# Opening the second feed-forward of a two-layer prefix-DiT: row sums on VectorE, weight remainders on GpSimd, a written-out order, and the two scale folds at set places

## The chip, the cores and the metric

One core of a Trainium2 chip runs the whole program, one launch per execution. The metric is the device time of one execution in microseconds (us). TensorE (PE in the profile) multiplies, VectorE (DVE), ScalarE (ACT) and GpSimd (POOL) do the elementwise work, SyncE (SP) issues the loads.

## What is computed

The model has two layers on 512 latent tokens (and 256 context tokens in the first layer), width 1024. Layer 0 mixes by attention, layer 1 by a gated recurrence (HGRN2); each mixer is followed by a SwiGLU feed-forward. Cut to what the change touches, which is the step from layer 1's mixer to its feed-forward:

```python
def rms_norm(x, w):
    y = x * lax.rsqrt(jnp.mean(x * x, axis=-1, keepdims=True) + NORM_EPS)
    return y * w
def modulate(h, shift, scale):
    return h * (1.0 + scale) + shift
def swiglu(h, w_in, w_out):              # w_in: 1024 x 5632, w_out: 2816 x 1024
    a, u = jnp.split(h @ w_in, 2, axis=-1)
    return (jax.nn.silu(a) * u) @ w_out
...
        h = h + gt1_l * y_l              # y_l ends with the product o @ w_o of the mixer
        h = h + gt2_l * swiglu(modulate(rms_norm(h, norm_ffn_w[i]), sh2_l, sc2_l),
                               ffn_w_in[i], ffn_w_out[i])
```

All inputs are float32.

## The kernel before, in words

**Layout.** Activations lie transposed: `hT[o]` is block o of eight, 128 channels on the partitions by tokens along the free axis. The 512 latent tokens of layer 1 are worked in two halves of H = 256 tokens, called half 0 and half 1.

**Products in three parts.** A float32 product is made of three products of a narrower type. `split` (L88) cuts an operand into a high part (a cast on ACT, L90) and a remainder, the low part (a subtraction on DVE or POOL, L95). `mm3` (L116) then issues high by high (L118), high by low of the moving operand (L119; the profile shows it as weight high with x low) and weight low by x high (L120).

**What stands at the change.** `hgrn_wo_last` (L1821) makes the last two of eight parts of the mixer's output product. For each half of the tokens it makes eight output rows, one per block o; in half 0 six of the rows have 3 matmuls left and two have 6, in half 1 each of the eight has 6, every matmul 256 tokens wide. Each row ends in `residual` (L760), one DVE instruction that reads the row from PSUM, scales it and adds it to `hT[o]`. It is a generator: each `next(pre)` emits one row.

`start_recurrence` (L1393), called once for layer 1, draws these rows and opens the feed-forward between them. For each half:

- **squares**: for each row, ACT squares the new `hT[o]` half (L274 for the first row, L278 for the others) and POOL adds the square to the running sum `acc_n` (L279), through two buffers, `sw`;
- **first fold** `rstd_cols` (L281): PE sums `acc_n` over its partitions (L285, tile `ssq`, two 128-token columns), DVE scales (L292), POOL raises to the power -1/2 (L294, tile `rc`);
- **second fold** `rstd_psum` (L297): DVE puts the 256 factors on diagonals (L300), PE multiplies them with ones (L304, tile `rstd`), so that each factor stands on all partitions in PSUM;
- **x** by `xhalf` (L1028): per block k, DVE multiplies `hT[k]` with the norm's weight and `rstd` (L1033), ACT adds the shift (L1035), ACT casts the high part and DVE (odd k) or POOL (even k) subtracts the low part; tiles `xw` for half 0, `xb12` and `xb22` for half 1;
- **products**: `plain(ps, j, i, k, h, ...)` (L1039) adds block k of hidden block j, i = 0 for the part under silu and 1 for the factor, to the PSUM tile `ffi`; three matmuls of 256 tokens each;
- **hidden** `plain_hidden` (L1055): silu on ACT, multiplication on DVE, and a split.

The weights of hidden blocks 0 and 1 come as four raw tiles (j, i) of 128 x 1024, loaded by SP into four ring buffers; `plain_split` (L1016) splits each. The low part of (0,0) is on POOL, those of (0,1), (1,0) and (1,1) on DVE. The order of the products in the program is: (0,0) and (0,1) of half 0 block by block, then (1,0) and (1,1) of half 0, then half 1.

**What sets the order.** A scheduler orders each engine's instructions when the kernel is built: by their place in the program, but an instruction whose inputs are ready earlier by the scheduler's own timing may go ahead. `pin(ins)` (L122) holds one instruction behind the one that was written before it on the same engine. Each engine then works its own list strictly in order and waits at the head of it. In the kernel before, the low parts of three weights are pinned here, and almost nothing else; the rows, the squares, the sums, the folds and x are placed by the scheduler.

## Time and profile before

| | |
|---|---|
| median of 3 runs | 1802.78 us (1802.26 to 1803.30) |
| the profiled execution's own time | 1803.39 us |
| its span in the profile | 1801.6 us |
| PE busy, of the span | 1747.4 us (97%) |
| DVE, ACT, POOL busy | 1306.6, 870.9, 641.0 us |
| mean granted PE clock | 0.993 |
| last row's product before the first fold, to the first product of x | 1424.57 to 1433.84 us |
| first product of half 1 | 1449.90 us |

Times inside the profile are counted from the start of the span. The profiled execution took 1803.39 us, 1.8 us more than its span and 0.6 us more than the median; a change in the span is taken as the same change in the time. In a row of the timeline stand: start, duration, engine, line, operation, output and inputs, shape, count, and in brackets the idle time before it with what ended it. A start is when the instruction began by the record; where an instruction then had to wait for a resource inside the chip, the wait lies within its duration. Rows with a count above 1 are merged neighbours. In a table of windows stand: the stretch, its length, the busy time of PE, PEld, DVE, ACT and POOL with the number of instructions, the granted PE clock (1.00 is full), and the DMA's share and rate.

### The profile page before, as it was taken

What the parts mean: (1) busy time and instruction counts of PE and PEld (TensorE: products, weight loads), DVE (VectorE), ACT (ScalarE), POOL (GpSimd) and SP (SyncE); (2) the same over time, 40 slices, a digit from 0 to 9 for tenths busy, and PEclk for the clock granted to TensorE, in tenths of its full rate; (3) what the DMA queues carried; (4) which work ended last, traced back from release to release, by engine and by line L of the source; (5) the groups of instructions that cost most, each with busy time, mean ns of one, the idle gap of its engine ahead of it and who ended that gap; (6) DMA issues with size and microseconds to landing.
All of it is one profiled execution on the core that took longest, in us unless ns stands there. A gap on an engine that the chain in (4) does not pass through costs nothing.

```text
span 1801.6 us, 30622 instructions
## 1 busy us (share of the span) xinstructions
PE 1747.4 (97%) x11717; PEld 1603.7 (89%) x11717; DVE 1306.6 (73%) x2269; ACT 870.9 (48%) x1777; POOL 641.0 (36%) x582
## 2 busy tenths in 40 slices
PE   9989999999999999999999999999999899999998
PEld 6788788998899989999998999898898899999996
DVE  4876688888988788888766555655747658786764
ACT  3544777767433514243446433334334545554544
POOL 1453445434513314132303243224425454333420
PEclk9999999999999999999999999999999899999999
DMA  9534400002134242545331212123211123333322
GB/s 339 177 114 139 142 25 24 25 1 77 36 111 118 65 135 83 164 132 161 94 106 46 70 61 77 54 71 94 71 48 47 56 59 115 100 115 100 100 61 83
DMA packets 213458, 166.43 MB, mean 92 GB/s; under 512 B 7952, under 2 KB 190400, under 8 KB 213312
## 3 DMA queue, kind: packets, MB, share of 16 engines
q1 hardware_dynamic: 213024, 163.43, 29.6%
q8 instruction: 92, 1.51, 0.3%
q10 hardware_dynamic: 288, 1.05, 0.1%
q14 instruction: 54, 0.44, 0.1%
HBM read 162.36 MB, written 2.10 MB: 91 GB/s over the span
## 4 chain that ended last, share of the span: by engine, by line
PE 77%; DVE 9%; ACT 4%; POOL 4%; issue 3%; DMA 2%; SPq 0%; POOLq 0%; DVEq 0%; ACTq 0%
PE ffo L120 5%; PE ffo L118 5%; PE ffo L119 5%; PE x L118 3%; PE x L120 3%; PE x L119 3%; PE pt L787 3%; PE lv L1716 3%; PE y L120 2%; PE y L118 2%; PE y L119 2%; PE hz L118 2%; PE hz L119 2%; PE hz L120 2%; PE sc L729 1%
## 5 line engine op out<-in xcount | busy, mean ns | idle before, releaser
L1723 POOL TENSOR_TENSOR KD<-KD,tot 128x384 f32<-128x384 f32 x96 | 102.3, 1088 | 81.7 <-ACT kc L1706 78.0
L777 POOL TENSOR_SCALAR pf<-pf,st 128x768 f32<-128x768 f32 (+1 forms) x96 | 73.3, 766 | 126.0 <-DVE st L776 89.5
L760 DVE SCALAR_TENSOR_TENSOR hT<-ffo,modc,hT 128x512 f32<-128x512 f32 (+1 forms) x122 | 78.6, 649 | 45.1 <-PE ffo L120 45.1
L120 PE MATMUL ffo<-gh,wlo_w 128*128 128x512 f32 (+1 forms) x304 | 102.7, 338 | 0.0
L119 PE MATMUL ffo<-gl,whi_w 128*128 128x512 f32 (+1 forms) x304 | 102.3, 336 | 0.0
L118 PE MATMUL ffo<-gh,whi_w 128*128 128x512 f32 (+1 forms) x304 | 101.8, 338 | 0.0
L242 DVE SCALAR_TENSOR_TENSOR adacc<-adw,csil,adacc 128x512 f32<-128x512 f32 x98 | 83.4, 861 | 8.9 <-DMA adw<-in_ada_w_dram 8.8
L95 DVE TENSOR_TENSOR ptl<-pt,pth 128x384 fp32r<-128x384 f32 (+1 forms) x160 | 79.9, 524 | 12.8 <-ACT pth L90 11.6
L90 ACT CAST pth<-pt 128x384 fp32r<-128x384 f32 (+1 forms) x160 | 69.7, 460 | 34.2 <-PE pt L787 22.4
L775 ACT ACTIVATE pf<-sc,st 128x768 f32<-128x768 f32 (+1 forms) x96 | 73.3, 764 | 18.9 <-DVE st L773 18.0
L1723 DVE TENSOR_TENSOR QD<-QD,tot 128x256 f32<-128x256 f32 x96 | 52.5, 587 | 41.4 <-PE lv L1716 41.2
L773 DVE TENSOR_REDUCE st<-sc 128x1 f32<-128x768 f32 (+1 forms) x96 | 74.1, 773 | 10.1 <-PE sc L730 8.7
L1706 ACT COPY kc<-KD 128x256 f32<-128x256 f32 x112 | 43.4, 414 | 75.6 <-PE lv L1716 46.2
L787 PE MATMUL pt<-ident,pf 128*128 128x128 f32 x448 | 72.1, 275 | 5.2 <-DVE ptl L95 3.8
L118 PE MATMUL ffo<-gh,foh 128*128 128x512 f32 (+1 forms) x186 | 71.5, 384 | 0.0
L120 PE MATMUL ffo<-gh,fol 128*128 128x512 f32 (+1 forms) x186 | 70.9, 381 | 0.2 <-DVE fol L95 0.2
L119 PE MATMUL ffo<-gl,foh 128*128 128x512 f32 (+1 forms) x186 | 70.9, 381 | 0.0
L1782 POOL TENSOR_SCALAR oss<-oss 128x4 f32<-128x4 f32 (+1 forms) x9 | 4.7, 523 | 182.8 <-DVE oss L1781 182.7
L1716 PE MATMUL lv<-QD,kc 128*128 128x128 f32 x448 | 64.1, 288 | 4.5 <-DVE QD L1723 2.4
L1716 PEld LDWEIGHTS lv<-QD,kc 128*128 128x128 f32 x448 | 59.5, 194 | 8.5 <-issue 4.3
L787 PEld LDWEIGHTS pt<-ident,pf 128*128 128x128 f32 x448 | 51.3, 140 | 13.8 <-issue 6.4
L119 PEld LDWEIGHTS ffo<-gl,whi_w 128*128 128x128 f32 x304 | 57.3, 188 | 6.8
(1114 smaller groups left out, 6801.7 us busy)
## 6 DMA issues: line engine op xcount, KB each, us to landing
adw<-in_ada_w_dram SPq DMA_DIRECT2D x40, 512.0 KB, 4.6
adw<-in_ada_w_dram SPq DMA_DIRECT2D x80, 256.0 KB, 3.0
raw_hz<-in_hgrn_w_in_dram SPq DMA_DIRECT2D x14, 512.0 KB, 3.7
adr<-in_ada_w_dram SPq DMA_DIRECT2D x16, 256.0 KB, 5.1
adr<-in_ada_w_dram SPq DMA_DIRECT2D x8, 512.0 KB, 8.5
raw_wq<-in_attn_w_qkv_dram SPq DMA_DIRECT2D x8, 512.0 KB, 4.9
raw_wo<-in_attn_w_o_dram SPq DMA_DIRECT2D x8, 512.0 KB, 3.4
raw_hv<-in_hgrn_w_in_dram SPq DMA_DIRECT2D x8, 512.0 KB, 4.6
```

What stands on the lines that cost most here:

```text
L95: m = (eng or DVE).tensor_tensor(lo, src, hi.bitcast(F32), op=ALU.subtract)
L118: PE.matmul(ps, ahi, bhi, start=first, stop=False, **kw)
L119: PE.matmul(ps, ahi, blo, start=False, stop=False, **kw)
L120: PE.matmul(ps, alo, bhi, start=False, stop=last, **kw)
L242: pin(DVE.scalar_tensor_tensor(a, raw, cc, a, op0=ALU.mult, op1=ALU.add))
L760: DVE.scalar_tensor_tensor(hT[o][:, a:e], ps, mcol(layer, ch, o, v), hT[o][:, a:e], op0=ALU.mult, op1=ALU.add)
L773: DVE.tensor_reduce(st3[:, 0:1], ps[:, :nk], op=ALU.max, axis=AX.X, negate=True)
L775: ACT.activation(pf, ps[:, :nk], AF.Exp, bias=st3[:, 0:1], accum_out=st3[:, 1:2])
L777: POOL.tensor_scalar(pf, pf, st3[:, 2:3], 1.0, op0=ALU.mult, op1=ALU.mult)
L787: PE.transpose(pt[:, i * P : (i + 1) * P], pf[:, (i0 + i) * P : (i0 + i + 1) * P], ident)
L1716: PE.matmul(ps[:, cs], kc[:, cs], mv, start=True, stop=True)
L1723: eng.tensor_tensor(view, view, f, op=ALU.mult)
```

## The change

- The squares of rows 1 to 7 of each half go to a new tile with three buffers, and the adding moves from POOL to DVE. It is written one or more rows behind: an add stands behind a later `residual` on DVE. Squares, adds, residuals are all pinned.
- The low parts of (0,1), (1,0) and (1,1) move from DVE to POOL, each cut into two instructions of 512 columns, and pinned.
- The first fold of half 0 is written after row 3 of half 1, the second after row 5; both are pinned on all their engines. Row starts of half 1 are pinned on PE.
- x of half 0 is written with its parts apart: the multiplication, the shift and the cast (`xfirst`), and one block later the low part (`xlow`), which is always on DVE, all pinned. Blocks 0 to 2 stand among rows 5 to 7, blocks 3 to 7 and the last two squares and five adds of half 1 stand among the products.
- The first fold of half 1 is written after the products (1,0) of half 0, the second after five of the eight blocks of (1,1).
- The second `plain_hidden` and the splits of weight block 2 are pinned.

```diff
@@ -113,9 +113,11 @@
-    def mm3(ps, ahi, alo, bhi, blo, first, last, onto=False):
+    def mm3(ps, ahi, alo, bhi, blo, first, last, onto=False, late=False):
         kw = dict(skip_group_check=True) if onto else {}
-        PE.matmul(ps, ahi, bhi, start=first, stop=False, **kw)
+        m = PE.matmul(ps, ahi, bhi, start=first, stop=False, **kw)
+        if late:
+            pin(m)
...
@@ -1013,36 +1021,60 @@
...
-        def plain_split(j, i, late=""):
+        def plain_split(j, i, late="", eng=None):
...
             pool_ = (j, i) == (0, 0) or j > 1 and i if layer else j == 0
-            split(t[0], t[1], raws.pop(("w", j, i)), POOL if pool_ else DVE, late=late)
+            raw = raws.pop(("w", j, i))
+            if eng is None:
+                split(t[0], t[1], raw, POOL if pool_ else DVE, late=late)
+            else:
+                ACT.copy(t[0], raw)
+                for c in (slice(0, 512), slice(512, 1024)):
+                    pin(eng.tensor_tensor(t[1][:, c], raw[:, c], t[0][:, c].bitcast(F32), op=ALU.subtract))
...
+        def xfirst(k, h, late=False):
             if k not in x:
                 x[k] = gslot((10 if layer else 2) + k, F32, f"x{k}")
             a0, e0 = halves[h][0][1], halves[h][-1][2]
             for v, a, e in halves[h]:
-                DVE.scalar_tensor_tensor(x[k][:, a:e], hT[k][:, a:e], a_c[:, k, v : v + 1], rst[h][:, a - a0 : e - a0],
-                                         op0=ALU.mult, op1=ALU.mult)
-                ACT.activation(x[k][:, a:e], x[k][:, a:e], AF.Identity, bias=mcol(layer, 3, k, v))
+                m = DVE.scalar_tensor_tensor(x[k][:, a:e], hT[k][:, a:e], a_c[:, k, v : v + 1], rst[h][:, a - a0 : e - a0],
+                                             op0=ALU.mult, op1=ALU.mult)
+                if late:
+                    pin(m)
+                m = ACT.activation(x[k][:, a:e], x[k][:, a:e], AF.Identity, bias=mcol(layer, 3, k, v))
+                if late:
+                    pin(m)
+            if late:
+                pin(ACT.copy(xops[("b1" if k < 4 else "b2") + "12"[h]][0][:, k % 4], x[k][:, a0:e0]))
+
+        def xlow(k, h):
+            a0, e0 = halves[h][0][1], halves[h][-1][2]
             xh, xl = xops[("b1" if k < 4 else "b2") + "12"[h]]
-            split(xh[:, k % 4], xl[:, k % 4], x[k][:, a0:e0], DVE if k % 2 else POOL)
-
-        def plain(ps, j, i, k, h, first, last):
+            pin(DVE.tensor_tensor(xl[:, k % 4], x[k][:, a0:e0], xh[:, k % 4].bitcast(F32), op=ALU.subtract))
+
+        def xsecond(k, h, eng):
+            a0, e0 = halves[h][0][1], halves[h][-1][2]
+            xh, xl = xops[("b1" if k < 4 else "b2") + "12"[h]]
+            split(xh[:, k % 4], xl[:, k % 4], x[k][:, a0:e0], eng)
...
@@ -1396,52 +1432,82 @@
             order = [0, 4, 1, 5, 2, 6, 3, 7]
             ps = [[{}, {}] for _ in range(nplain)]
 
-            def products(j, h, i, ks):
+            def products(j, h, i, ks, late=False):
                 for k in ks:
-                    plain(ps[j][i], j, i, k, h, k == 0, k == KT - 1)
-
-            for h in range(2):
+                    plain(ps[j][i], j, i, k, h, k == 0, k == KT - 1, late and k == ks[0])
+
+            sums = []
+
+            def square(h, o):
                 hs = slice(h * H, (h + 1) * H)
-                for i in range(KT):
-                    o = next(pre)
-                    sumsq_add(acc_n[:, hs], fp, hT[o][:, hs], o, i == 0, POOL, tag="sw", bufs=2, width=512)
-                    if h == 0 and i == 0:
-                        plain_split(0, 0, "l")
-                    if h == 0 and i == KT - 1:
-                        plain_split(0, 1, "l")
-                    if h == 1 and i == 1:
-                        plain_split(1, 0, "l")
-                    if h == 1 and i == 2:
-                        rst[0] = rstd_psum(ctile("c22", 2), rc[0], H)
-                    if h == 1 and i >= 4:
-                        xhalf(i - 4, 0)
-                rc[h] = rstd_cols(fp, acc_n[:, hs], H, f"rc{h}")
+                if o == 0:
+                    pin(ACT.activation(acc_n[:, hs], hT[o][:, hs], AF.Square))
+                    return
+                sq = fp.tile([P, H], F32, tag="sqo", bufs=3, name="sqo")
+                pin(ACT.activation(sq, hT[o][:, hs], AF.Square))
+                sums.append((acc_n[:, hs], sq))
+
+            def add():
+                acc, sq = sums.pop(0)
+                pin(DVE.tensor_tensor(acc, acc, sq, op=ALU.add))
+
+            plain_split(0, 0, "l")
+            for i in range(KT):
+                square(0, next(pre))
+                if len(sums) > 1:
+                    add()
+                if i in (1, 4):
+                    plain_split(*((0, 1) if i == 1 else (1, 0)), "l", POOL)
+            for i in range(KT):
+                o = next(pre)
+                if i == 0:
+                    add()
+                if i < 6:
+                    square(1, o)
+                if i == 3:
+                    rc[0] = rstd_cols(fp, acc_n[:, 0:H], H, "rc0", late=True)
+                    plain_split(1, 1, "l", POOL)
+                if i in (3, 4):
+                    add()
+                if i == 5:
+                    rst[0] = rstd_psum(ctile("c22", 2), rc[0], H, late=True)
+                if i >= 5:
+                    xfirst(i - 5, 0, True)
+                if i == KT - 1:
+                    xlow(0, 0)
             for _ in pre:
                 pass
             for _ in range(2):
                 load_next()
             for k in range(KT):
-                if k >= 4:
-                    xhalf(k, 0)
+                if 0 < k < 6:
+                    xfirst(k + 2, 0, True)
+                if k < KT - 1:
+                    xlow(k + 1, 0)
+                if k in (1, 3):
+                    square(1, 6 if k == 1 else 7)
+                if 0 < k < 6:
+                    add()
                 for i in range(2):
                     products(0, 0, i, [k])
-            plain_split(1, 1, "l")
-            rst[1] = rstd_psum(ctile("c22", 2), rc[1], H)
+            hidden_tiles(0)
+            hidden_tiles(1)
+            products(1, 0, 0, range(KT))
+            rc[1] = rstd_cols(fp, acc_n[:, H:n], H, "rc1", late=True)
+            products(1, 0, 1, range(5), True)
+            rst[1] = rstd_psum(ctile("c22", 2), rc[1], H, late=True)
+            products(1, 0, 1, range(5, KT), True)
             for k in order[:2]:
                 xhalf(k, 1)
-            hidden_tiles(0)
-            hidden_tiles(1)
-            for i in range(2):
-                products(1, 0, i, range(KT))
             plain_hidden(0, 0, *ps[0])
             for k in order[2:]:
                 xhalf(k, 1)
-            plain_hidden(1, 0, *ps[1])
+            plain_hidden(1, 0, *ps[1], late=True)
             for i_, k in enumerate(order):
                 for i in range(2):
                     plain(ps[0][i], 0, i, k, 1, i_ == 0, i_ == KT - 1)
-            plain_split(2, 0)
-            plain_split(2, 1, "l")
+            plain_split(2, 0, "hl")
+            plain_split(2, 1, "hl")
...
@@ -1850,8 +1916,8 @@
                     ps, todo = both[:, (o - 6) * 256 : (o - 6) * 256 + 256], (0, 1)
                 for i in todo:
                     mm3(ps, wo[i][0][:, osl], wo[i][1][:, osl], os_[i][0][:, a:e], os_[i][1][:, a:e],
-                        i == 0, i == 1, True)
-                residual(o, ps, 1, 2, 0, a, e)
+                        i == 0, i == 1, True, h == 1 and i == 0)
+                pin(residual(o, ps, 1, 2, 0, a, e))
                 yield o
 
     NSTEP = 14
```

What is cut from the diff passes `late` on to the folds and to `plain_hidden`, so that their instructions are pinned, and returns the instruction of `residual`.

More of the change, by code (lines that the diff above doesn't have):

```diff
@@ L287, in rstd_cols, with rstd_of @@
                 pin(m)
-        return rstd_of(pl, pc, nt, tag)
-    def rstd_of(pl, pc, nt, tag="rc"):
+        return rstd_of(pl, pc, nt, tag, late)
+    def rstd_of(pl, pc, nt, tag="rc", late=False):
         rc = pl.tile([P, NT], F32, tag=tag, name="rc")[:, :nt]
-        DVE.tensor_scalar(rc, pc[:, 0 : 2 * nt].rearrange("p (t v) -> p t v", v=2)[:, :, 0], 1.0 / D, EPS,
+        m = DVE.tensor_scalar(rc, pc[:, 0 : 2 * nt].rearrange("p (t v) -> p t v", v=2)[:, :, 0], 1.0 / D, EPS,
                           op0=ALU.mult, op1=ALU.add)
-        POOL.tensor_tensor(rc, rc, mhalf.to_broadcast([P, nt]), op=ALU.pow)
+        if late:
+            pin(m)
+        m = POOL.tensor_tensor(rc, rc, mhalf.to_broadcast([P, nt]), op=ALU.pow)
+        if late:
+            pin(m)
         return rc
@@ L299, in rstd_psum @@
         dg = dg[:, 0:n].rearrange("p (t q) -> p t q", q=P)
-        DVE.tensor_tensor(dg, ident.unsqueeze(1).to_broadcast([P, nt, P]), rc.unsqueeze(2).to_broadcast([P, nt, P]),
+        m = DVE.tensor_tensor(dg, ident.unsqueeze(1).to_broadcast([P, nt, P]), rc.unsqueeze(2).to_broadcast([P, nt, P]),
                           op=ALU.mult)
+        if late:
+            pin(m)
         ps = bank("rstd")[:, 0:n]
@@ L759, in residual @@
     def residual(o, ps, layer, ch, v, a, e):
-        DVE.scalar_tensor_tensor(hT[o][:, a:e], ps, mcol(layer, ch, o, v), hT[o][:, a:e], op0=ALU.mult, op1=ALU.add)
+        return DVE.scalar_tensor_tensor(hT[o][:, a:e], ps, mcol(layer, ch, o, v), hT[o][:, a:e], op0=ALU.mult, op1=ALU.add)
     ap_ = pool("att", att)
@@ L1028, in xhalf @@
         def xhalf(k, h):
+            xfirst(k, h)
+            xsecond(k, h, DVE if k % 2 else POOL)
+        def xfirst(k, h, late=False):
             if k not in x:
@@ L1044, in plain @@
                 ps[h] = xbank("ffi")[:, 0:H]
-            mm3(ps[h], hi[:, c], lo[:, c], xh[:, k % 4], xl[:, k % 4], first, last)
+            mm3(ps[h], hi[:, c], lo[:, c], xh[:, k % 4], xl[:, k % 4], first, last, late=late)
         gh, gl = {}, {}
@@ L1053, in hidden_tiles, with plain_hidden @@
             gl[j] = gslot(at + 1, F32R, f"gl{jj}")
-        def plain_hidden(j, h, psa, psu):
+        def plain_hidden(j, h, psa, psu, late=False):
             c = ctile("c22", 2)
-            ACT.activation(c, psa[h], AF.Silu)
-            DVE.tensor_tensor(c, psu[h], c, op=ALU.mult)
-            split(gh[j][:, h * H : h * H + H], gl[j][:, h * H : h * H + H], c)
+            m = ACT.activation(c, psa[h], AF.Silu)
+            if late:
+                pin(m)
+            m = DVE.tensor_tensor(c, psu[h], c, op=ALU.mult)
+            if late:
+                pin(m)
+            split(gh[j][:, h * H : h * H + H], gl[j][:, h * H : h * H + H], c, late="hl" if late else "")
         def xsplit(m, i, src, eng=DVE, late=""):
```

6 lines of the change are left out of this document (added).

## The prediction

> **What bounds the kernel now.** I read the page first, then who PE waited for from 1390 to 1520 us, then a table of windows, then the timeline there.
>
> ```profile
> PE 1747.4 (97%) x11717; PEld 1603.7 (89%) x11717; DVE 1306.6 (73%) x2269; ACT 870.9 (48%) x1777; POOL 641.0 (36%) x582
> ```
>
> PE carries the kernel, so a change pays only where PE is idle or slowed. In the opening it waits four times, and the windows show that the first wait costs more than its length:
>
> ```profile
> PE ssq L285 <- POOL acc_n L279: 3.2, 1, 3.2
> PE ffi L118 <- ACT xw L90: 1.8, 1, 1.8
> PE ffi L119 <- POOL xw L95: 0.6, 1, 0.6
> PE ffi L119 <- DVE xw L95: 0.3, 1, 0.3
> ```
>
> ```profile
> 474.78:478.19 3.41, 2.65 (x8) 2.42 (x9) 3.19 (x6) 2.27 (x5) 0.00 (x0) 0.50 0.00 0
> 478.19:481.61 3.42, 3.38 (x11) 2.57 (x10) 2.61 (x6) 3.09 (x8) 0.00 (x0) 0.50 0.52 153
> 1382.73:1386.14 3.41, 1.82 (x8) 0.95 (x7) 3.41 (x4) 1.02 (x3) 2.88 (x3) 1.00 0.24 70
> 1386.14:1389.55 3.41, 3.41 (x17) 3.41 (x17) 3.41 (x9) 0.59 (x1) 0.18 (x1) 0.50 0.30 89
> 1423.69:1427.10 3.41, 1.15 (x10) 0.95 (x8) 1.30 (x2) 1.92 (x5) 3.17 (x4) 1.00 0.59 172
> 1427.10:1430.51 3.41, 2.44 (x11) 2.44 (x12) 0.96 (x4) 0.89 (x3) 2.36 (x5) 0.50 0.47 135
> 1430.51:1433.93 3.42, 1.65 (x9) 1.35 (x7) 2.63 (x8) 2.12 (x6) 2.35 (x4) 0.50 0.01 2
> 1433.93:1437.34 3.41, 3.41 (x16) 3.41 (x17) 2.79 (x8) 3.10 (x10) 2.98 (x5) 0.50 0.00 0
> 1437.34:1440.75 3.41, 2.93 (x25) 2.72 (x23) 1.41 (x4) 2.46 (x9) 1.87 (x4) 1.00 0.00 0
> ```
>
> The granted clock holds one value per slice of 3.41 us. A slice in which PE was busy 1.82 us or less is followed by one at 0.50; one at 0.50 with 2.65 us busy (474.78) is followed by another at 0.50, one with 3.41 us (1433.93) is not. Here three slices run at half speed. PE is busy 2.44 + 1.65 + 3.41 = 7.5 us in them, and half of that, 3.75 us, is lost. With the waits, 5.9 us, the opening holds 9.7 us (0.5%) to be won at most. What can be told from no change by a measurement of this kernel is about 0.2%, 3.6 us.
>
> Where the first wait comes from:
>
> ```profile
> 1417.81 1.04 ACT L90 CAST w01h<-raw_('w', 0, 1)_14886 128x1024 fp32r<-128x1024 f32 x1
> 1418.74 1.05 ACT L90 CAST w11h<-raw_('w', 1, 0)_14888 128x1024 fp32r<-128x1024 f32 x1
> 1418.34 3.83 DVE L760 SCALAR_TENSOR_TENSOR hT<-hwo,modc,hT 128x256 f32<-128x256 f32 x9
> 1419.69 0.42 ACT L274 ACTIVATE acc_n<-hT 128x256 f32<-128x256 f32 x1
> 1420.01 0.71 ACT L278 ACTIVATE sq<-hT 128x256 f32<-128x256 f32 x2
> 1420.49 8.21 POOL L279 TENSOR_TENSOR acc_n<-acc_n,sq 128x256 f32<-128x256 f32 x8 [2.23 <-ACT sq L278]
> 1428.07 1.01 PE L285 MATMUL ssq<-ones,acc_n 128*128 128x2 f32 x4 [3.23 <-POOL acc_n L279]
> ```
>
> Residuals follow each other at 3.83 / 9, about 0.4 us; POOL's adds take 8.21 / 8 = 1.03 us, and PE stands before the fold for 3.23 us, from 1424.84 to 1428.07. Its idle time ends when the sum does.
>
> **The change, part by part.** *The sums.* On DVE an add of two SBUF tiles has the form of a low part: 0.41 us, the next 0.33 us later. But that is its price alone:
>
> ```profile
> 1448.64 0.41 DVE L95 TENSOR_TENSOR xb12l<-x,xb12h 128x256 fp32r<-128x256 f32 x1
> 1448.97 0.42 DVE L95 TENSOR_TENSOR xb22l<-x,xb22h 128x256 fp32r<-128x256 f32 x1
> 1451.13 2.65 POOL L95 TENSOR_TENSOR wlo_w<-raw_('w', 2, 1)_15083,whi_w 128x1024 fp32r<-128x1024 f32 x1
> 1451.44 2.62 DVE L95 TENSOR_TENSOR xb22l<-x,xb22h 128x256 fp32r<-128x256 f32 x1
> 1415.87 2.39 POOL L95 TENSOR_TENSOR wlo_w<-raw_('w', 0, 0)_14884,whi_w 128x1024 fp32r<-128x1024 f32 x1
> ```
>
> The same low part that took 0.42 us took 2.62 us when POOL's weight remainder had begun 0.3 us before it, and ended 0.28 us after that one ended. So the two exclude each other for a whole instruction. Residuals do not: nine ran at 0.4 us each while POOL was adding. The change puts just this beside the adds: four POOL halves of 2.39 / 2 = 1.2 us for (0,1) and (1,0), free to start when their casts end, at 1418.85 and 1419.79.
>
> The Trainium skill (SBUF — State Buffer, Who interferes with whom) has it as a rule: a DVE instruction with two SBUF inputs and a GpSimd one that reads SBUF hold the shared port one at a time, and the second blocks until the first ends; it speaks against this change, and the 2.62 us agree.
>
> DVE's list is now residual 0, 1, 2, add 1, residual 3, add 2 and so on. Square 1 ends at 1420.43 and add 1 is next, but POOL is in its second half (1420.1 to 1421.3): add 1 at 1421.3. Behind a waiting add stand the next residual and ACT's next square; PE's rows wait for neither. POOL's third half then takes 1421.6 to 1422.85, add 2 follows; the fourth ends at 1424.4, add 3 follows, at 1424.7. Then four more residual-and-add pairs of 0.4 + 0.335, 2.9 us: the sum stands at **1427.7**, 0.3 us before now. Without exclusion it would stand at 1425.4. I take 1427.7, because the exclusion is in the rows; both ends stay.
>
> PE meets this earlier than before. The fold stands after row 3 of half 1: 30 + 24 row matmuls from 1417.15 (the first after the last head's product) at 0.1175 us end at 1423.5. The wait is 4.2 us for 3.2, and the slice 1423.69 to 1427.10 is empty, so the clock falls again.
>
> *From the first fold to x.* Prices, at half speed where it is PE:
>
> ```profile
> 1417.15 0.71 PE L118 MATMUL hwo<-oth,whi_hwo 128*128 128x256 f32 x4
> 1449.78 0.28 PE L120 MATMUL ffi<-xw,w11l 128*128 128x256 f32 x1
> 1449.90 0.28 PE L118 MATMUL ffi<-xb12h,whi_w 128*128 128x256 f32 x1
> 1430.16 0.41 PE L120 MATMUL hwo<-oth,wlo_hwo 128*128 128x256 f32 x1
> 1430.37 0.41 PE L118 MATMUL hwo<-oth,whi_hwo 128*128 128x256 f32 x1
> 1429.36 0.71 POOL L294 TENSOR_TENSOR rc<-rc,mhalf 128x2 f32<-128x2 f32 x1 [0.66 <-DVE rc L292]
> 1430.10 0.43 DVE L300 TENSOR_TENSOR c<-ident,rc 128x256 f32<-128x256 f32 x1 [0.43 <-POOL rc L294]
> 1431.01 1.06 PE L304 MATMUL rstd<-c,ones 128*128 128x128 f32 x4
> 1432.11 0.48 DVE L1033 SCALAR_TENSOR_TENSOR x<-hT,a_ffn,rstd 128x256 f32<-128x256 f32 x1 [0.79 <-PE rstd L304]
> 1433.84 0.58 PE L118 MATMUL ffi<-xw,whi_w 128*128 128x256 f32 x1 [1.77 <-ACT xw L90]
> ```
>
> Now 4.0 us lie between fold and x (1428.07 to 1432.11). After: the first fold 0.8, rows 4 and 5, twelve matmuls at 0.213 = 2.6, so row 5 ends at about 1431.5; its residual, pinned ahead of the diagonals, 0.5; the diagonals 0.43 with up to 0.6 of waiting for a POOL half of (1,1), which starts right after the power: 1432.9; the second fold 1.06: **x at 1433.9**. The pinned residual hides the power's 0.71, but itself costs the path. Rows 6 and 7, twelve more at 0.213, stand behind the second fold and hold PE until 1436.4; products of x begin there, where they began at 1433.84.
>
> *Products of half 0.* DVE now does per block x 0.4, low part 0.335 and add 0.335 = 1.07 us; the low part of block 7 ends at 1444.5. On ACT the two late squares lie between casts; a block costs ACT 0.40 + 0.30 and has 1.07, so they are hidden, at 0.3 us each if it had not. PE has 72 matmuls, 8.5 us, in the same 8 us when (1,0) is drawn forward, so DVE's price is hidden, and PE's own work decides: from 1437.9 (x 1 and 2 wait on DVE behind the residuals of rows 6 and 7, then comes the first low part) 94 matmuls, 11.0, and two folds, 0.9, make 1449.8 at full clock. The clock recovers at 1437.34, at 1440.75 or at 1444.2, by whether the 2.8 us or so of busy time in a slice are enough (the rows leave that open between 2.65 and 3.41); half of the time from 1437.9 is lost. So (1,1) ends at 1449.8, 1451.2 or 1452.9; now it ends at 1449.90, where half 1 begins. Taken: the middle one, **+1.3 us**, since 2.8 is nearer to 2.65 in the first slice and the next is full.
>
> *Second fold of half 1.*
>
> ```profile
> 1444.14 0.61 PE L304 MATMUL rstd<-c,ones 128*128 128x128 f32 x4
> 1447.03 0.91 ACT L1035 ACTIVATE x<-x,modc 128x256 f32<-128x256 f32 x2
> 1447.84 0.39 ACT L90 CAST xb12h<-x 128x256 fp32r<-128x256 f32 x1
> 1446.59 0.75 POOL L95 TENSOR_TENSOR xb12l<-x,xb12h 128x256 fp32r<-128x256 f32 x1 [4.92 <-ACT xb12h L90]
> ```
>
> Now this fold is 5.8 us ahead of half 1's first product (1449.90), and x of half 1 is made under (1,0) and (1,1). After, nine matmuls, 1.06 us, are left behind it. From its start to the first low part: 0.61 + 0.48 + 0.51 + 0.39 + 0.75 and four hand-overs of about 0.05 = 2.9 us, against 1.5 of PE work, the fold's own and the nine. PE then takes a block in 0.7 us, ACT makes one in 0.40 + 0.30, so it doesn't catch up: **+1.4 us**. Zero would need x earlier than its fold; the upper end is 4 us, if DVE takes x and low parts in the written order, where four blocks' low parts wait 1.0 us each (0.51 + 0.39 and hand-overs) for their cast, with the next x behind them.
>
> *The rest.* The 512-column cut, the third buffer and the pins add no work. Casts of (2,0) and (2,1) move behind the second hidden block, but their product begins about 11 us later than half 1's, against a cast of 1.05 and a remainder of 2.65: nothing. If that cover were gone they would cost 3.7. The loads of (2,0) to (3,1) follow the freed raw tiles: (2,1) now follows POOL's (0,1), 3 us earlier; nobody waits. Removed from DVE are three remainders of 1.2 us, which now hide no more than the waits of the adds.
>
> Sum: 1.3 + 1.4 = +2.7 us on 1803.39 is 1806.1; the profiled execution lies 0.6 above the median, so **1805.5**.
>
> **Rivals.** *A: POOL is not in the way* (its halves run earlier, or yield). The sum stands at 1425.4. For: POOL is idle from 1418.26 (1415.87 + 2.39) to 1420.49. Against: the casts end at 1418.85 and 1419.79. PE then waits 1.9 us, the slice to 1427.10 is busy 1.5 us, less than 1.82, and the clock falls at 1427.10, when most of rows 4 and 5 is done: x at 1429.7, rows 6 and 7 to 1432.1, the first low part at 1433.6, then 11.9 of work and 1.9 for half speed until 1437.34: 1447.4, -2.5 + 1.4 = -1.1, **1801.7**. *B: A, and the clock stays.* The sum comes half a microsecond sooner, or the slices lie otherwise; rows 6 and 7 take 1.4, the first low part stands at 1432.1, and 11.9 later it is 1444.0: -5.9 + 1.4 = -4.5, **1798.3**. The point that decides is 1.82 us of busy time in the slice in which the fold waits. The Trainium skill (TensorE: Matmul & The Clock Gate, HAM oscillation — how this bites in real kernels) asks only that no gap exceed about 3.4 us; by it, A would be B. The slice at 1382.73, with 1.6 us idle, was followed by half clock, so the row decides.
>
> *C: half 1 starves.* Beside the forecast's +1.3, x of half 1 costs the upper 4, and its gaps bring a slice at 0.50 in which PE works half of the time, 0.9: +6.2, **1809.0**. It decides from 1.6 us idle in a slice there. For: one fold with 1.06 us of cover. Against: x there is not pinned. *D: the pins don't hold what the text says.* Casts stay free; misplaced, one costs 0.95 us on ACT: within the forecast's own range.
>
> **How the numbers follow.** Forecast (with D) 0.47, its own range 1804.1 to 1807.2 (+1.3 to +4.4), about two thirds of it below +3.6: same 0.30, slower 0.17. A 0.13, same. B 0.20, faster. C 0.20, slower. So faster 0.20, same 0.43, slower 0.37. The range reaches from B's price to C's and just beyond: 1798.0 to 1809.5; the far halves of B and C, 2 in 10, are left out.
>
> **What would show it.** Right: PE waits about 4 us for the fold on DVE's `acc_n` (L279's new line); some of DVE's adds last 0.8 to 1.5 us and end 0.3 us after a POOL half; clock 0.50 from 1427.1 for four slices or so; x about 1434; PE waits over a microsecond after the second fold of half 1. Wrong: adds of 0.42 us throughout, or a fold reached before 1425, or a full clock from 1423 to 1440.

## The result, and the profile after

The changed kernel takes 1811.47 us (median of 6 runs, 1808.83 to 1814.37); the kernel before 1802.95 us in the same comparison (6 runs, 1802.26 to 1805.75). The ratio is 1.0046 with a 95% interval of 1.0035 to 1.0056: slower by 6.3 to 10.1 us. Forecast were 1805.5 us and, eight times in ten, 1798.0 to 1809.5. The forecast's sum has the direction right and the size wrong: it is +2.7 us, and the range ended at +6.7. Of the three outcomes it held likeliest, at 0.43, a change too small to be told from none.

The profiled execution took 1809.67 us (span 1807.9 us, before 1801.6). In it the last head ends 1.30 us earlier in the span than before, so start times of the two traces are set side by side from there and not from the span's start. The page's first part after:

```profile
PE 1749.3 (97%) x11717; PEld 1603.1 (89%) x11717; DVE 1314.7 (73%) x2284; ACT 873.8 (48%) x1777; POOL 635.2 (35%) x570
```

Nothing is to be seen there: PE has the same instructions and 97% as before. The list of whom PE waits for, from 1390 to 1520 us (engine, line, releaser: us in total, times, longest):

```profile
PE hwo L118 <- DVE hT L768: 6.1, 2, 5.5
PE rstd L312 <- DVE c L306: 2.6, 1, 2.6
PE ffi L118 <- ACT xb12h L90: 0.8, 1, 0.8
PE ffi L121 <- DVE xw L1064: 0.7, 1, 0.7
...
PE ffi L121 <- POOL xb12l L95: 0.2, 1, 0.2
```

Before, the opening held 5.9 us of waits, now 10.3. Forecast was a wait of some 4 us at the first fold for `acc_n`. There is none. In its place stands one of 5.5 us that the forecast does not have: a product of a row of the output projection (`hwo`) waits for a residual (L768). The timeline of PE, DVE and POOL at that place (start, us, engine, line; in brackets the idle time ahead and what ended it):

```profile
1417.62 2.53 POOL L1037 TENSOR_TENSOR w01l<-raw_('w', 0, 1)_14886,w01h 128x512 fp32r<-128x512 f32 x2 [0.67 <-ACT w01h L1035]
1418.65 0.28 PE L122 MATMUL hwo<-oth,wlo_hwo 128*128 128x256 f32 x1
1419.15 1.28 DVE L1452 TENSOR_TENSOR acc_n<-acc_n,sqo 128x256 f32<-128x256 f32 x1 [0.85 <-ACT sqo L1447]
1420.11 2.86 POOL L1037 TENSOR_TENSOR w11l<-raw_('w', 1, 0)_14888,w11h 128x512 fp32r<-128x512 f32 x2
1420.75 1.08 DVE L1452 TENSOR_TENSOR acc_n<-acc_n,sqo 128x256 f32<-128x256 f32 x1
1422.15 1.09 DVE L1452 TENSOR_TENSOR acc_n<-acc_n,sqo 128x256 f32<-128x256 f32 x1
1423.56 0.41 DVE L1452 TENSOR_TENSOR acc_n<-acc_n,sqo 128x256 f32<-128x256 f32 x1
1423.89 0.47 DVE L768 SCALAR_TENSOR_TENSOR hT<-hwo,modc,hT 128x256 f32<-128x256 f32 x1
1424.42 0.58 PE L118 MATMUL hwo<-oth,whi_hwo 128*128 128x256 f32 x1 [5.49 <-DVE hT L768]
```

The first three adds take 1.1 to 1.3 us, for as long as POOL's halves run, and the fourth 0.41 us when they have ended: so far the forecast. But PE stops at 1418.9, 24 matmuls after the last head's product, and goes on when the residual at 1423.89 has ended. It is the residual of row 6 of half 0, and the matmul is the first of row 7. Rows 6 and 7 lie in the two halves of one PSUM bank (`both`), so row 7 is not begun before row 6 has been read. The residual stands on DVE behind four adds, and three of them behind POOL.

The table of windows, cut at the steps of the clock (busy us of PE, PEld, DVE, ACT and POOL, each with its instructions, then the granted clock):

```profile
1419.08:1422.49 3.41, 0.00 (x0) 0.00 (x0) 3.34 (x5) 2.23 (x6) 3.41 (x3) 1.00 0.90 266
1422.49:1425.90 3.41, 1.48 (x7) 1.48 (x8) 2.20 (x5) 1.53 (x4) 0.47 (x1) 0.50 0.79 229
1425.90:1429.32 3.42, 3.42 (x18) 3.42 (x18) 2.12 (x5) 0.91 (x3) 0.00 (x0) 0.50 0.09 24
...
1432.73:1436.15 3.42, 1.28 (x10) 1.22 (x10) 2.56 (x4) 0.43 (x2) 1.80 (x2) 1.00 0.07 17
1436.15:1439.56 3.41, 2.47 (x11) 2.00 (x9) 1.84 (x5) 1.87 (x5) 0.00 (x0) 0.50 0.46 137
1439.56:1442.97 3.41, 3.11 (x14) 3.12 (x15) 3.41 (x10) 3.13 (x8) 0.00 (x0) 0.50 0.00 0
1442.97:1446.39 3.42, 3.42 (x31) 3.42 (x30) 3.09 (x9) 3.20 (x8) 0.00 (x0) 1.00 0.00 0
```

A whole slice without a matmul, four slices at half speed where there were three. The second gap, at 1432.7, is the second fold, and half 1 has one of its own (same timeline):

```profile
1431.86 2.67 POOL L1037 TENSOR_TENSOR w11l<-raw_('w', 1, 1)_14890,w11h 128x512 fp32r<-128x512 f32 x2
1433.73 1.09 DVE L306 TENSOR_TENSOR c<-ident,rc 128x256 f32<-128x256 f32 x1
1434.87 0.71 PE L312 MATMUL rstd<-c,ones 128*128 128x128 f32 x4 [2.60 <-DVE c L306]
1454.23 0.39 PE L118 MATMUL ffi<-xb12h,whi_w 128*128 128x256 f32 x1 [0.76 <-ACT xb12h L90]
```

The diagonals (`c`, L306) take 1.09 us where they had taken 0.43, until POOL's half of (1,1) is done.

One difference is in no list of waits. From the first unit's first product to the end the two kernels run the same instructions, and PE waits there for the same 2.7 us. First the kernel before, then the changed one:

```profile
core 0 of [0], span 1801.6 us
1484.36 0.28 PE L118 MATMUL x<-xw,whi_w 128*128 128x256 f32 x1
```

```profile
core 0 of [0], span 1807.9 us
1489.39 0.28 PE L118 MATMUL x<-xw,whi_w 128*128 128x256 f32 x1
```

That leaves 317.24 us before and 318.51 after, 1.27 us more, spread evenly over the whole stretch. The same table for every kernel of this study, H being the start of the last head's transpose that PE has waited 0.47 or 0.48 us for (1415.28 before, 1413.98 after), P the first product of half 1, U the first of the first unit; "half" counts the slices at clock 0.50 in the opening:

| kernel | median us | ratio to before (95%) | H to P | H to U | U to end | half |
|---|---|---|---|---|---|---|
| before | 1802.95 | 1 | 34.62 | 69.08 | 317.24 | 3 |
| after | 1811.47 | 1.0046 (1.0035 to 1.0056) | 40.25 | 75.41 | 318.51 | 4 |
| 1 fills on GpSimd | 1806.60 | 1.0022 (1.0012 to 1.0032) | 36.55 | 71.69 | 318.53 | 2 |
| 2 a bank each | 1806.47 | 1.0026 (1.0017 to 1.0035) | 36.08 | 71.23 | 318.44 | 3 |
| 3 both | 1805.33 | 1.0011 (1.0001 to 1.0020) | 35.17 | 70.32 | 318.47 | 3 |
| 4 adds alone | 1803.35 | 1.0007 (0.9999 to 1.0016) | 35.36 | 69.82 | 317.09 | 2 |
| 5 places alone | 1804.88 | 1.0010 (1.0001 to 1.0019) | 34.00 | 68.49 | 318.81 | 2 |
| 6 casts late | 1803.38 | 1.0003 (0.9994 to 1.0012) | 31.53 | 66.69 | 318.64 | 2 |
| 7 folds early | 1810.30 | 1.0046 (1.0034 to 1.0059) | 39.79 | 74.29 | 318.50 | 4 |
| 8 low half late | 1802.46 | 0.9996 (0.9987 to 1.0005) | 35.53 | 69.99 | 317.34 | 4 |
| 9 old places | 1798.81 | 0.9979 (0.9968 to 0.9991) | 31.15 | 65.81 | 317.35 | 2 |
| 10 cover | 1799.67 | 0.9979 (0.9969 to 0.9989) | 30.76 | 65.41 | 317.43 | 0 |
| 11 rows free | 1807.23 | 1.0019 (1.0010 to 1.0029) | 36.67 | 71.83 | 318.47 | 3 |
| 12 late alone | 1811.97 | 1.0037 (1.0024 to 1.0051) | 40.57 | 75.73 | 318.65 | 4 |

The ratio goes against runs of the kernel before on the same chip, whose median moved between 1802.9 and 1804.8 us, so kernels are compared by it. The three stretches come from one execution each.

### The profile page after: what moved, and what is told of

It is laid out like the page before. It is cut to its first block, busy times and chain, and to the rows that moved or that the text cites. A ratio compares the mean times of both kernels' runs of the same rounds, so it can differ in the third digit from the quotient of the medians.

```text
span 1807.9 us, 30615 instructions
## 1 busy us (share of the span) xinstructions
PE 1749.3 (97%) x11717; PEld 1603.1 (89%) x11717; DVE 1314.7 (73%) x2284; ACT 873.8 (48%) x1777; POOL 635.2 (35%) x570
## 4 chain that ended last, share of the span: by engine, by line
PE 79%; DVE 9%; ACT 4%; issue 3%; POOL 2%; DMA 2%; SPq 0%; POOLq 0%; ACTq 0%; DVEq 0%
PE ffo L122 5%; PE ffo L121 5%; PE ffo L118 5%; PE x L118 3%; PE x L121 3%; PE x L122 3%; PE pt L795 3%; PE y L121 2%; PE y L122 2%; PE y L118 2%; PE lv L1782 2%; PE hz L118 2%; PE hz L121 2%; PE hz L122 2%; PE sc L737 1%
## 5 line engine op out<-in xcount | busy, mean ns | idle before, releaser
L768 DVE SCALAR_TENSOR_TENSOR hT<-ffo,modc,hT 128x512 f32<-128x512 f32 (+1 forms) x122 | 78.5, 648 | 46.0 <-PE ffo L122 46.0
```

The costliest lines, as they stand in the source:

```text
L768: return DVE.scalar_tensor_tensor(hT[o][:, a:e], ps, mcol(layer, ch, o, v), hT[o][:, a:e], op0=ALU.mult, op1=ALU.add)
```

## The experiments

Theory: three causes, the shared bank with the pinned rows, GpSimd's halves, and the little cover of half 1's fold. Main rival: the order itself costs the time, and a wait taken away comes back at the next place.

**2. A bank each for rows 6 and 7.**

```diff
-            both = bank("hwo") if h == 0 else None
...
-                    both = both or xbank("hwo")
-                    ps, todo = both[:, (o - 6) * 256 : (o - 6) * 256 + 256], (0, 1)
+                    both = bank("hwo") if h == 0 else xbank("hwo")
+                    ps, todo = both[:, 0:256], (0, 1)
```

> The changed kernel with rows 6 and 7 of each half in a PSUM bank each, in place of one that they share. Theory, that the shared bank is why PE stood at row 7: the 5.49 us there are gone, PE runs on to row 3 of half 1 and waits about 4 us at the first fold for the sum, the clock falls once less or later, and the time falls by 3 to 6 us against the changed kernel, to 1805 to 1808, which is the course that the prediction had. Rival, that DVE's chain of residuals and adds sets the pace whatever PE does ahead: the wait only moves from row 7 to the fold and the time changes by less than 1 us.

The list of waits of this kernel:

```profile
PE ssq L287 <- DVE acc_n L1452: 4.4, 1, 4.4
PE rstd L312 <- DVE c L306: 1.3, 1, 1.3
PE ffi L118 <- ACT xb12h L90: 0.8, 1, 0.8
PE ffi L121 <- DVE xw L1064: 0.7, 1, 0.7
```

The wait at row 7 is gone, and PE waits 4.39 us at the fold, where the forecast had 4.2. H to U is 4.2 us shorter than in the changed kernel, and the ratio falls from 1.0046 to 1.0026. The theory holds: the bank was worth about 4 us, mainly, as the trace is read here, because with it 30 row matmuls (row 7 and rows 0 to 3 of half 1) were left for the time after the wait, at half speed.

**11. The rows of half 1 free.** Did the bank do it, or the pins that fixed row 7's place?

```diff
-                        i == 0, i == 1, True, h == 1 and i == 0)
+                        i == 0, i == 1, True)
```

> The changed kernel without the pins on the first product of half 1's rows, so that the planner again chooses where row 7 of half 0, which waits for row 6's residual, stands among them: in the program built so it stands behind 29 matmuls of rows 0 to 4 of half 1. Theory, that the shared bank cost its 5.5 us because the pins had put row 7 ahead of all those rows: 29 matmuls at 0.1175 are 3.4 us, so the wait at row 7 falls to about 2.1 us, and the time falls by 2 to 5 us against the changed kernel, about as with a bank each. Rival, that PE then only waits the same time at the folds: within 1 us of the changed kernel.

```profile
PE hwo L118 <- DVE hT L768: 3.2, 4, 1.3
PE rstd L312 <- DVE c L306: 2.6, 1, 2.6
```

Row 7 now stands behind 29 matmuls of half 1. The waits for residuals are 3.2 us in four places, 1.3 at the longest, where 2.1 in one was expected; H to U is 3.6 us shorter and the ratio 1.0019. So both are needed for the 5.5 us: the bank ties row 7 to a residual, and the pins put it ahead of everything that could have covered it. In the kernel before the bank was shared too, but its free planner had put 12 matmuls of half 1 ahead of row 7, and no add stood on DVE.

**1. Fills in place of GpSimd's halves.**

```diff
-                    pin(eng.tensor_tensor(t[1][:, c], raw[:, c], t[0][:, c].bitcast(F32), op=ALU.subtract))
+                    pin(eng.memset(t[1][:, c].bitcast(F32), 0.0))
```

> The changed kernel with the six GpSimd halves of the weight low parts (0,1), (1,0) and (1,1) replaced by fills with zero, which write SBUF and read none; left out is the share of those low parts in the products. Theory, that GpSimd's halves hold DVE's adds and the adds hold the residual of row 6, on which row 7 waits because both share a PSUM bank: every add lasts 0.42 us or less, the residual of row 6 ends about 2 us earlier, PE's wait at row 7 is 3 to 4 us where it was 5.49, the wait at the second fold of half 0 is about 1 us where it was 2.60, and the time falls by 3 to 5 us against the changed kernel, to about 1807. Rival, that the pinned order itself and not the exclusion costs the time: the adds may be short, but the time changes by less than 1 us.

The time fell by about as much as expected (1.0046 to 1.0022), but not at row 7. The adds are 0.42 us and the wait at the second fold is 0.93 (2.60 in the changed kernel), both as expected; the wait at row 7 is still 5.03 us where 3 to 4 were expected, and the rest of the gain stands in the clock (two slices, not four). ACT's and DVE's timeline says what took GpSimd's place:

```profile
1424.81 0.51 ACT L90 CAST foh<-raw_('fo', 0, 0)_15540 128x384 fp32r<-128x384 f32 x1 [1.54 <-DMA raw_('fo', 0, 0)_15540<-in_ffn_w_out_dram]
1425.23 0.41 ACT L1447 ACTIVATE sqo<-hT 128x256 f32<-128x256 f32 x1
1425.67 0.43 DVE L1452 TENSOR_TENSOR acc_n<-acc_n,sqo 128x256 f32<-128x256 f32 x1 [1.55 <-ACT sqo L1447]
```

A cast of the output weights, which nobody needs for a long time, stands in ACT's list ahead of square 4 and waits 1.54 us for its load; the add behind that square waits 1.55 us, and behind the add the residual that row 7 waits for.

**12. Those casts late, nothing else.** In the changed kernel they should be hidden behind GpSimd.

```diff
-            split(g[0], g[1], u["src"](), late=("l" if layer or nsplit[0] < 2 else "hl") if begun[0] else "")
+            split(g[0], g[1], u["src"](), late=("hl" if layer or nsplit[0] >= 2 else "l") if begun[0] else "")
```

> The changed kernel with the two casts of the output weights alone pinned behind the squares. Theory, that in the changed kernel they are hidden, since DVE stands behind GpSimd's halves meanwhile, and show only once GpSimd is out of the way (third and sixth experiment): the wait at row 7 stays between 5.2 and 5.5 us, and the time within 1 us of the changed kernel. Rival, that they hold the squares here too: the wait falls by 1 us or more.

The wait at row 7 is 5.49 us, to the hundredth as in the changed kernel, H to U is 75.73 for 75.41, and the intervals of the two ratios overlap. The theory holds. Of two engines that hold the same chain, the one that ends first is free.

**3. Fills and a bank each.** The edits of 1 and 2 together.

> Fills in place of the six GpSimd halves (the same low parts left out) and a bank each for rows 6 and 7. Theory: the sum stands about 2 us earlier, PE waits 1 to 2 us at the first fold and hardly at row 7 or at the second fold; 1798 to 1803, the case that the prediction had as its rivals A and B. If the pinned order itself costs the time it stays above 1807.

1805.33 us, above the 1798 to 1803 expected and below 1807. The fold still waits 3.87 us, for `acc_n`: the sum stands behind the two casts, which wait 1.08 and 0.96 us for their loads. So with GpSimd out of the way neither of the forecast's faster rivals comes about.

**6. Fills, a bank each, casts late.** The edits of 1, 2 and 12 together.

> The third experiment (fills in place of GpSimd's halves, a bank each for rows 6 and 7) with the two casts of the output weights on ACT pinned to their place in the text, far behind the squares. Theory, that with GpSimd out of the way ACT's squares 4 and 5 stood behind these casts, which stood waiting for their loads: the sum is ready about 2 us earlier, PE's wait at the first fold falls from 3.87 to between 1.5 and 2.2 us, and the time falls by 1.5 to 4 us against the third experiment, most if the clock then stays up. Rival, that DVE's chain of eight residuals and seven adds sets the sum by itself: the wait stays above 3 us and the time within 1 us of the third experiment.

```profile
PE ssq L287 <- DVE acc_n L1452: 1.6, 1, 1.6
PE rstd L312 <- DVE c L306: 0.9, 1, 0.9
```

1.62 us, within the 1.5 to 2.2 expected; H to U is 3.6 us shorter than in 3. By the ratios the gain is 1.4 us (0.0008), with intervals that would allow anything from a loss of 1 to a gain of 4. Here the forecast's rival A is seen for the first time: it had put this wait at 1.9 us.

**4. The adds alone, in the kernel before.**

```diff
-                    sumsq_add(acc_n[:, hs], fp, hT[o][:, hs], o, i == 0, POOL, tag="sw", bufs=2, width=512)
+                    sumsq_add(acc_n[:, hs], fp, hT[o][:, hs], o, i == 0, DVE, tag="sw", bufs=2, width=512)
```

> The kernel before with one part of the change alone: the squares added on DVE, everything else as it was. Adds of 0.4 us take the place of GpSimd's 1.03 us, GpSimd then has only the remainder of (0,0) in that stretch. Theory, that DVE's adds are good where no weight remainder runs on GpSimd: PE's first wait of 3.2 us becomes 1.5 us or less, and the time falls by 1 to 3 us against the kernel before. Rival, that adds on DVE are bad in themselves, because they stand between the residuals: the time rises by 1 us or more.

The wait at the fold is 1.15 us (3.23 before), yet the time is the same: ratio 1.0007, interval 0.9999 to 1.0016. The second fold now waits 3.13 us. POOL's and DVE's timeline:

```profile
1426.12 1.22 DVE L95 TENSOR_TENSOR w01l<-raw_('w', 0, 1)_14886,w01h 128x1024 fp32r<-128x1024 f32 x1
1427.49 2.28 POOL L294 TENSOR_TENSOR rc<-rc,mhalf 128x2 f32<-128x2 f32 x1 [9.83 <-DVE rc L292]
1427.66 1.21 DVE L95 TENSOR_TENSOR w11l<-raw_('w', 1, 0)_14888,w11h 128x1024 fp32r<-128x1024 f32 x1
```

The power, 0.71 us before, takes 2.28 us beside DVE's remainders: the exclusion works in this direction as well, and experiment 8, which takes one of them away, has 0.81. The expected gain of 1 to 3 us did not come.

**8. The adds, with that remainder moved and the casts late.** To experiment 4 come experiment 12's edit and:

```diff
-                    if h == 1 and i == 1:
-                        plain_split(1, 0, "l")
...
             for _ in pre:
                 pass
+            plain_split(1, 0, "l")
```

> The kernel before with the squares added on DVE (the fourth experiment), the low half of (1,0) moved behind the rows, so that GpSimd's power does not stand beside it, and the two casts of the output weights pinned behind the squares. Nothing of the computation is left out. Theory: the wait at the first fold falls from 1.15 us to 0.3 or less, the power from 2.28 us to about 0.8, the wait at the second fold from 3.13 us to about 1.6; the time falls by 2 to 5 us against the kernel before, 1798 to 1801, most if the clock stays up. Rival, that the waits only move on to the first products: within 1 us of the kernel before.

The fold no longer waits, the power is 0.81 us and the second fold waits 1.63, all as expected; the time is not (0.9996, 0.9987 to 1.0005). The first products wait 2.0 us, a new wait of 0.69 us, for (1,0)'s low half, stands in the products, and the clock falls twice. The rival was right: the waits moved on.

**7. Half 1's folds half a product earlier.**

```diff
-            products(1, 0, 0, range(KT))
+            products(1, 0, 0, range(4))
             rc[1] = rstd_cols(fp, acc_n[:, H:n], H, "rc1", late=True)
-            products(1, 0, 1, range(5), True)
+            products(1, 0, 0, range(4, KT), True)
             rst[1] = rstd_psum(ctile("c22", 2), rc[1], H, late=True)
-            products(1, 0, 1, range(5, KT), True)
+            products(1, 0, 1, range(KT), True)
```

> The changed kernel with both folds of half 1 earlier by half a product: the first after four of the eight blocks of product (1,0,0), the second ahead of product (1,0,1), so that 24 matmuls and not 9 stand behind the second. Theory, that those nine matmuls are too little cover for the chain from the fold to half 1's x: the waits of 0.76 and 0.20 us at half 1's first products are gone, and the time falls by 1.0 to 1.5 us against the changed kernel. Rival, that ACT and DVE have no room there and are the bound: the wait stays, no change.

The waits of 0.76 and 0.20 us are gone and H to U is 1.12 us shorter, as expected. The ratio is the same as the changed kernel's, 1.0046 with an interval of about 2 us to each side: it neither shows 1.1 us nor speaks against it.

**5. The changed kernel's places in SBUF, in the kernel before.** The tiles are allocated early, in the other order, and the squares in buffers of their own:

```diff
-                    sumsq_add(acc_n[:, hs], fp, hT[o][:, hs], o, i == 0, POOL, tag="sw", bufs=2, width=512)
+                    sumsq_add(acc_n[:, hs], fp, hT[o][:, hs], o, i == 0, POOL, tag="sqo", bufs=3, width=H)
...
+                    if h == 0 and i == 1:
+                        for slot, key in ((3, (0, 1)), (1, (1, 0)), (0, "rc0"), (2, (1, 1))):
...
```

> The kernel before, with nothing changed but the places of its tiles in SBUF: the second feed-forward's tiles are allocated in the order and sizes of the changed kernel, so that each stands at the changed kernel's address. Every kernel with the change's tiles (the changed kernel and the first three experiments) took 1.2 to 1.3 us longer than the kernel before from the first unit to the end, spread evenly, though the instructions there are the same. Theory, that this comes from the addresses: this kernel's opening is as before, and from the first unit to the end it takes 318.4 to 318.6 us where the kernel before took 317.24; in all +1.2 us. Rival, that it comes from the state in which the opening leaves the chip: 317.1 to 317.4 us there, and no difference in all.

```profile
core 0 of [0], span 1804.0 us
1485.19 0.28 PE L118 MATMUL x<-xw,whi_w 128*128 128x256 f32 x1
```

318.81 us from U to the end, 1.57 more than before, with the opening's waits nearly as before (3.2, 1.8, 0.6, and 0.3 new at the second fold). In all 1.0010 (1.0001 to 1.0019), +0.2 to +3.4 us. The theory holds: the new places, which come from the third buffer and the new order of allocation together and which the forecast had at nothing, cost over a microsecond far behind the change.

**10. A version by all this.** Nothing is left out. Edits of 2, 7 and 12, and in the opening:

```diff
-                if i in (1, 4):
-                    plain_split(*((0, 1) if i == 1 else (1, 0)), "l", POOL)
...
-                if i == 3:
+                if i == 4:
                     rc[0] = rstd_cols(fp, acc_n[:, 0:H], H, "rc0", late=True)
-                    plain_split(1, 1, "l", POOL)
-                if i in (3, 4):
+                if i in (4, 5):
                     add()
                 if i == 5:
-                    rst[0] = rstd_psum(ctile("c22", 2), rc[0], H, late=True)
-                if i >= 5:
-                    xfirst(i - 5, 0, True)
+                    dg0 = rstd_diag(ctile("c22", 2), rc[0], H, late=True)
+                    plain_split(0, 1, "l")
+                if i == 6:
+                    rst[0] = rstd_fold(dg0, H, late=True)
+                if i >= 6:
+                    xfirst(i - 6, 0, True)
```

Here `rstd_diag` and `rstd_fold` are the two halves of `rstd_psum`; (1,0)'s low half follows block 3 and (1,1)'s the last block, both on DVE, and x's first parts stand one row later, among the blocks too (that line is left out above).

> The changed kernel with what the runs so far point to, nothing of the computation left out: rows 6 and 7 in a bank each; the casts of the output weights behind the squares; no weight low half on GpSimd, the one of (0,1) on DVE behind the diagonals, those of (1,0) and (1,1) on DVE among and behind the blocks; the first fold of half 0 one row later and its second fold behind row 6; half 1's folds half a product earlier. Theory: PE waits 1 us or less at the first fold and at the second, about 1 us at the first products, and the clock stays up or falls for two slices at most; from the last head's product to half 1's first product 28 to 30 us where the kernel before took 32.8, and 1797 to 1801 in all, with the later stretch still 1.2 us longer than before. Rival, that DVE, which now carries all low halves and adds, becomes the bound of the products of half 0: waits of over 2 us there, and 1802 or more.

```profile
PE ffi L118 <- ACT xw L1066: 1.5, 1, 1.5
PE rstd L319 <- DVE c L309: 1.2, 2, 0.9
PE ssq L287 <- DVE acc_n L1459: 0.9, 1, 0.9
```

The waits are shared out, 0.9, 0.9 and 1.5 us; the clock does not fall in the opening of the profiled execution. About 1 us was expected for the third wait. H to P is 30.76 us, 3.9 less than before, and the ratio 0.9979 (0.9969 to 0.9989): faster than both kernels, by 2.0 to 5.6 us against before. One thing missed: U to the end is 317.43 us, not 318.4 to 318.8. This order of allocation puts the tiles at a third set of addresses, though the third buffer is kept, and that set costs 0.2 us in all.

**9. The same with the old places.** As 10, the tiles allocated early in the order of the kernel before, and the squares' buffers as halves of its two:

```diff
-                sq = fp.tile([P, H], F32, tag="sqo", bufs=3, name="sqo")
+                if "sq" in early:
+                    sq = early.pop("sq")
+                else:
+                    t = fp.tile([P, 2 * H], F32, tag="sw", bufs=2, name="sqo")
+                    sq, early["sq"] = t[:, 0:H], t[:, H : 2 * H]
```

> The tenth experiment with the second feed-forward's tiles back at the addresses that they have in the kernel before (the squares' buffers as halves of two tiles, the others allocated in the old order). Theory, that the addresses cost 1.2 us from the first unit to the end: 317.1 to 317.4 us there, where the tenth experiment takes 318.4 to 318.8, and 1.2 us less in all, 1796 to 1800. Rival: no difference there.

U to the end is 317.35 us and the ratio again 0.9979. Here the rival holds, since 10 had nothing to give back. Not every move of the tiles costs, then; the changed kernel's does, in eight traces of kernels with its places and in experiment 5 by itself (318.4 to 318.8, against 317.1 to 317.4 in the five others). Taking tiles back one by one was not tried. The traces narrow it: against the kernel before, all nine lose 0.89 to 0.91 us in the 558 output products (`ffo`) and 0.39 or 0.40 in the 216 products of `y` with `xt1`; 10 loses 0.66 in the first and next to nothing in the second, and gains 0.37 in those of `x` with `xt3`. Experiment 9, with the old places, loses 0.20 in the first, which is about the scatter.

## Why the prediction was wrong

**The failed step** is this one: "Behind a waiting add stand the next residual and ACT's next square; PE's rows wait for neither." Row 7 waits for the residual of row 6, by the bank that they share, and the pins put row 7 ahead of all of half 1's rows. So PE did not run on to the fold and reach it at 1423.5, as the forecast has it, but stood at row 7 for 5.49 us. Experiment 2 takes that one thing away and has the forecast's picture: wait at the fold 4.39 us (forecast 4.2), three slices at half speed (four). H to P is 1.46 us longer than before, 0.75 of it the wait ahead of P, and P to U 0.69 us: (1,1) ends 0.7 us later (forecast 1.3), and half 1 takes 1.4 us more (forecast 1.4). Sum to the first unit: +2.15 us for +2.7. (One sum of the forecast is off: 1427.7, 0.8 and 2.6 make 1431.1 for the end of row 5, not 1431.5. With it the forecast would have been 0.2 to 0.4 us lower.) The step could have been seen in the code: `both` is one tile for two rows. The Trainium skill (PSUM — Partial Sum Buffer, PSUM bank collisions raise a hardware error) has it that two engines may not touch one bank at the same time and that the schedule has to keep them apart, halves or not; the 5.49 us agree.

**"The 512-column cut, the third buffer and the pins add no work"** is true of the work, but the sum had no term for where the tiles come to lie: 1.27 us by the places in SBUF (experiment 5 shows it for buffer and order of allocation together; 10 keeps the buffer and does not lose it). So the profiled executions give 6.33 us from H to U and 1.27 from U to the end, 7.6 us, within the interval of 6.3 to 10.1: 2.15 of it the forecast's own terms, 4.2 bank and pins, 1.27 places.

**GpSimd's exclusion** was right in size: adds of 1.28, 1.08 and 1.09 us, 0.41 without a half beside them, and 0.42 throughout with fills. The same holds for the diagonals behind (1,1): forecast up to 0.6 us of waiting, measured 0.66 (1.09 for 0.43).

**Rivals A and B** did not come true, since GpSimd was in the way, and could not have come true for a second reason that the forecast did not see: with GpSimd out of the way the output weights' casts hold ACT's squares (experiments 1 and 3). Only with three things changed (6) did A's wait stand there.

**Half 1's fold** with nine matmuls behind it was right: 0.76 and 0.20 us of waits, gone in experiment 7, with 1.12 us in the trace.

**The clock** fell for four slices, as forecast, but in two pairs, from 1422.49 and from 1436.15 us, and the rule by busy time does not hold, as is shown below.

## What to carry to other kernels

When an engine's list is pinned and gets a slower instruction, go through everything that is queued behind it and ask who reads or overwrites the same PSUM bank; a bank shared by two rows makes the matrix engine wait for the vector engine, and pins can put that wait ahead of all work that would cover it. A term that hides behind a longer one is not gone: take the longer away and the next holder (here a cast waiting for a load) stands there. Several waits of about 1 us can cost less than one of 4: the same three waits brought no slice at half speed in experiment 10 and two in 9, where the kernel before has three. The slices lay otherwise on them: the first of these waits ended 1.53 us into a slice in 9 and 2.75 us in 10.

## What was not expected of the hardware

**In this opening the clock goes by streamed columns, not by busy time.** The prediction read the step to 0.50 from PE's busy time in a slice of 3.41 us: 1.82 us or less. Slices of experiment 5 and then of experiment 8 speak against that:

```profile
1424.58:1428.00 3.42, 1.68 (x15) 1.47 (x13) 1.82 (x3) 2.42 (x7) 3.19 (x4) 1.00 0.57 158
1428.00:1431.41 3.41, 1.77 (x13) 1.57 (x13) 0.90 (x4) 0.66 (x2) 2.81 (x5) 1.00 0.53 150
```

```profile
1433.05:1436.46 3.41, 2.49 (x17) 1.87 (x15) 2.40 (x7) 3.41 (x9) 1.36 (x2) 1.00 0.00 0
1436.46:1439.88 3.42, 2.79 (x13) 2.79 (x14) 3.42 (x7) 2.65 (x7) 2.65 (x3) 0.50 0.40 121
1439.88:1443.29 3.41, 3.41 (x18) 3.41 (x18) 2.19 (x3) 0.73 (x1) 0.78 (x1) 0.50 0.64 187
```

In 5 the slice that was busy 1.68 us is not followed by one at half speed, and the next, busy 1.77 us, is (from 1431.41). In 8 a slice at full speed that was busy 2.49 us is followed by one at half speed. What sorts them is the number of columns that the slice's matmuls stream: 256 for a row or a product, 128 for a diagonal, 2 for a matmul of a fold's sums, each counted in the slice in which it starts. The slice of 5 that is not followed by half speed has 3072, the other 2312, and the first of 8 has 2824. Over the slices that begin between H and P in all 14 traces, 35 with 2824 columns or fewer were each followed by 0.50 and all with 3584 or more by 1.00; of seven at 3072 to 3328 three were followed by 0.50. The bound lies there at either speed, so at half speed 14 of the 16 products that fit were enough (the changed kernel's slice at 1439.56, x14), 12 or 13 not always; at full speed some 29 fit. The Trainium skill (TensorE: Matmul & The Clock Gate, HAM oscillation — how this bites in real kernels) asks only for no gap over about 3.4 us; the longest wait in experiment 9's opening is 1.47 us and the clock fell.

The count describes this stretch, in which nearly all matmuls are 256 columns wide, and not the chip. Elsewhere in the same traces, where many are 128 wide, it fails: experiment 10's slice from 1386.87 us has 1536 columns and is followed by 1.00, experiment 8's from 95.03 us has 4096 and is followed by 0.50. What the chip goes by stays open. Records missing from a trace make such counts a little uncertain.

**Places in SBUF.** The same matmuls ran 0.4% slower for 317 us (1.27 of 317.24) with the changed kernel's addresses, with no wait in the list; experiment 5, which has the changed kernel's addresses and otherwise the kernel before, shows that they suffice.
